# Additions to x on VectorE, one block sum to an item, and the first weights of a run split inside the run before it

## The chip, the cores and the metric

The kernel runs on one core of a Trainium2 chip. The metric is the device time of one execution in microseconds (us), the median of three runs for the kernel before. Five engines run side by side, each through its own list of instructions in order: TensorE (PE in the profile; its weight loads are PEld) multiplies into PSUM banks, VectorE (DVE) and ScalarE (ACT) work on SBUF and PSUM, GpSimd (POOL) works on SBUF and issues the DMAs that add while they write, SyncE (SP) issues the plain DMAs. Instructions of different engines wait for each other by semaphores.

## The reference

A two-layer encoder of 512 positions, width 1024, in float32. Each layer is attention and a SwiGLU feed-forward part, each behind an RMSNorm and added to x; a last RMSNorm ends it. Layer 0 has windowed attention with grouped keys, layer 1 a mixture of three dilated groups. The change touches the feed-forward part alone:

```
def swiglu(h, w_gate, w_up, w_down):
    return (jax.nn.silu(h @ w_gate) * (h @ w_up)) @ w_down

        h = rmsnorm(x, norm_ffn[i])
        x = x + swiglu(h, w_gate[i], w_up[i], w_down[i])
```

D_FF is 2816, which is 22 chunks of 128 hidden units. x is held transposed, as eight tiles of 128 features by 512 positions.

## The kernel before

**Products in three parts.** Every float32 operand is split into a high part in TensorE's rounded format and a low part, the rest (`split`, L92: ScalarE copies the high part, VectorE subtracts it from the source). A product is then three matmuls: high by high, high by low, low by high (`mm3`, L121; `product`, L738). A matmul has 128 rows of contraction, 128 outputs and 256 positions.

**The feed-forward part** is `swiglu` (L601). It runs twice, for layer 0 and for layer 1, with the same code:

- `conventional` (L892) makes hidden chunks 0 to 5 (PLAIN is 6) in the plain way.
- *Run 0* makes chunks 6 to 21 (L945): 16 items, each a gate and an up chunk together.
- *Run 1* (L946) multiplies chunks 6 to 13 by the down weights: four items of two output tiles of x (0 and 1, 2 and 3, 4 and 5, 6 and 7).
- *Run 2* (L947) does the same with chunks 14 to 21 for three items, output tiles 0 to 5.
- The *plain down products* (`down_plain`, L861) multiply chunks 0 to 5 for each of the eight output tiles; one tile is six chunk steps of six matmuls each. They come in three lots (L949): tiles 0 to 3 (24 chunk steps), 4 to 6 (18), and 7 (6). A lot begins at the end of a run and ends in the next.
- The *tail* (`tail`, L965) multiplies chunks 14 to 21 for output tiles 6 and 7 without the scheme below, with weights that `split_tail` (L985) prepares.

**An item** is a two by two block product done with seven block products rather than eight (the Strassen-Winograd scheme). Its operands on the side of the positions are B11, B21, B22 and the sums T1 to T4, made once for a run by `less` (VectorE, 1024 columns, L659) and split into the slots of bh and bl by `parts` (L655). On the side of the weights they are w1 to w7, made for every item by `weights` (L706). A pair of weights is loaded (`load_pair`, L701; SP); sums of weights are made by two plain DMAs and two accumulating ones (`load_sums`, L691; SP and GpSimd). From them come, by name: h12 and l12 (high and low parts of w1, w2), h64 and l64 (w6, w4), f5 and f7 (two sums on VectorE, 512 columns each, L725), h57 and l57 (w5, w7), `last` (a load of half a weight, L729), h3 and l3 (w3). The letters h are copies on ScalarE (L715), the letters l subtractions on VectorE (L721), of 1024 columns but for h3 and l3 with 512. The tiles wraw, wh and wl have three buffers each (L73), shared by pairs, by w1 w2, by w6 w4 and by the plain weights; the tile gs has two, and so has the sum of weights' h57 and l57; the sums have three.

**The order of work** is written out step by step in `strassens` (L811) and holds for TensorE, VectorE and ScalarE (L885, L990); the framework arranges SP and GpSimd. A step t has one block product. Item k's products w1 w2 w5 w4 w6 w3 w7 stand at steps 7k + 0, 1, 3, 5, 6, 9, 11, so neighbouring items interleave and each step of the middle has just one. The two banks of an item are a (tag mm, three buffers) and b (tag sc, two). Around the products, counted from the item's first step (L788):

- 1, 4, 7: ScalarE copies bank a to gs, to gs again, to us (L754); each copy must be done before the next product goes into bank a
- 8: `add`, VectorE adds part of bank b to us (L765), ahead of w7, which goes on in that part
- 12: `gate`, VectorE adds bank b to gs (L768); for a down item gs is then added to tile j of x: by GpSimd in run 1, by VectorE in run 2 (L774)
- 13: `both`, VectorE makes the other two blocks; for a down item it takes them into tile j + 1 of x (L785)

The weights of item k + 1 are made through item k's steps by the tables MAKE and MAKE_FIRST (L804, L808): for the second item of a run h12 at step 2, l12 and f5 at 3, f7 and h64 at 4, h57 and l64 at 5, l57 at 6, h3 at 10, l3 at 11; for later items h12 at the item's first step, l12 after it, then h64 and f5, l64, f7, h57, l57 at 2 to 6.

**Where runs meet** (from L1000). At the end of a run, steps without a product are filled with chunk steps of the plain lot that begins there: three at step `end`, then three at each of the last three steps (L849). The first weights of runs 1 and 2 are made after the last step, with chunk steps of the plain lot between them (eight ahead of run 1, four ahead of run 2, L1004 to L1011), and the rest of the lot (four, two) stands at step 2 of the new run (L839). The block sums of run 1 are made in the last steps of run 0 (L995 to L998), those of run 2 at steps 11, 14, 18 and 21 of run 1 (L1015). In `final` (L527), after the last layer, the tail's products are followed by the last norm and the outputs.

## Time and profile before

| | |
|---|---|
| median of three runs | 1389.37 us (1387.91 to 1391.34) |
| the profiled execution | 1389.48 us |
| its span, first to last instruction | 1387.7 us |
| mean granted TensorE clock | 0.998 |
| run 0's last step with w7 to the tail, layer 0 | from about 400 to 505 us |
| the same in layer 1 | from about 1259 to 1364 us |

The profile is that of one execution. A row of a timeline has the start, the duration, the engine, the line of the kernel, the operation and its tiles, output before input, and in brackets how long the engine had been idle before it and what ended that. Consecutive instructions of an engine overlap a little, so what one costs is read from start to start. A row of the waits view has the waiting engine and line, what it waited for, the total in us, the number of times and the longest. A row of the stretches has the busy time of each engine and its instructions, the granted clock and the DMA engines' share and GB/s. A row of the chain has a start, a duration and the work that the end of the kernel hung on there.

### The profile page before, as it was taken

What the parts mean: (1) busy time and instruction counts of PE and PEld (TensorE: products, weight loads), DVE (VectorE), ACT (ScalarE), POOL (GpSimd) and SP (SyncE); (2) the same over time, 40 slices, a digit from 0 to 9 for tenths busy, and PEclk for the clock granted to TensorE, in tenths of its full rate; (3) what the DMA queues carried; (4) which work ended last, traced back from release to release, by engine and by line L of the source; (5) the groups of instructions that cost most, each with busy time, mean ns of one, the idle gap of its engine ahead of it and who ended that gap; (6) DMA issues with size and microseconds to landing.
All of it is one profiled execution on the core that took longest, in us unless ns stands there. A gap on an engine that the chain in (4) does not pass through costs nothing.

```text
span 1387.7 us, 29649 instructions
## 1 busy us (share of the span) xinstructions
PE 1369.9 (99%) x12246; PEld 1352.1 (97%) x12246; DVE 960.0 (69%) x1699; ACT 726.7 (52%) x1304; POOL 262.2 (19%) x354
## 2 busy tenths in 40 slices
PE   9999999999999999999999999999999999999997
PEld 8988999999999999999999999999999999999997
DVE  6876558877779886345555555646466887778976
ACT  6766434555554567335545436436344555555543
POOL 1244220121202031011111111211132021210305
PEclk9999999999999999999999999999999999999999
DMA  6110263787747332322222122222136288774621
GB/s 204 62 62 16 77 176 103 188 204 186 191 134 183 103 104 78 108 79 91 70 84 91 64 92 78 77 84 70 63 107 175 92 213 199 189 194 137 169 88 62
DMA packets 67111, 164.63 MB, mean 119 GB/s; under 512 B 8992, under 2 KB 11424, under 8 KB 66976
## 3 DMA queue, kind: packets, MB, share of 16 engines
q1 hardware_dynamic: 51904, 137.95, 30.7%
q0 software_dynamic: 14784, 24.27, 10.8%
q8 instruction: 96, 1.57, 0.5%
q10 hardware_dynamic: 288, 0.52, 0.1%
q14 instruction: 39, 0.32, 0.1%
HBM read 160.53 MB, written 2.17 MB: 117 GB/s over the span
## 4 chain that ended last, share of the span: by engine, by line
PE 87%; DVE 6%; ACT 3%; issue 2%; DMA 1%; SPq 0%; POOL 0%; DVEq 0%; ACTq 0%; POOLq 0%
PE mm L126 31%; PE mm L742 16%; PE sc L742 12%; PE psv L126 9%; PE tp L126 6%; PE sc L126 2%; PE ov L447 1%; PE sc L1191 1%; PE ovb L1246 1%; PE sc L1132 1%; PE tp L1154 1%; ACT pr L423 1%; PE mm L973 1%; DVE pr L416 1%; PE ov L1173 1%
## 5 line engine op out<-in xcount | busy, mean ns | idle before, releaser
L98 DVE TENSOR_TENSOR wl<-wraw,wh 128x1024 fp32r<-128x1024 f32 (+4 forms) x154 | 179.2, 1166 | 106.8 <-ACT wh L97 103.9
L126 PE MATMUL mm<-xh,wh 128*128 128x256 f32 x1120 | 226.2, 283 | 0.5 <-ACT xh L260 0.5
L97 ACT ACTIVATE wh<-wraw 128x1024 fp32r<-128x1024 f32 (+4 forms) x153 | 149.3, 981 | 138.9 <-PE mm L126 101.3
L126 PE MATMUL mm<-xl,wh 128*128 128x256 f32 x1120 | 219.7, 278 | 0.3 <-DVE xl L261 0.3
L126 PE MATMUL mm<-xh,wl 128*128 128x256 f32 x1120 | 219.6, 277 | 0.0
L126 PEld LDWEIGHTS mm<-xh,wh 128*128 128x128 f32 x1120 | 169.9, 189 | 2.4 <-ACT xh L260 0.8
L126 PEld LDWEIGHTS mm<-xl,wh 128*128 128x128 f32 x1120 | 169.2, 188 | 1.0 <-DVE xl L261 1.0
L126 PEld LDWEIGHTS mm<-xh,wl 128*128 128x128 f32 x1120 | 169.0, 188 | 0.2 <-DVE wl L98 0.2
L698 POOL DMA_DIRECT2D w<-wunits x92 | 80.5, 918 | 442.7 <-DVE l L721 176.4
L742 PE MATMUL mm<-bh,h 128*128 128x256 f32 x368 | 102.3, 278 | 4.2 <-ACT gs L754 4.2
L742 PE MATMUL mm<-bh,l 128*128 128x256 f32 x368 | 102.3, 278 | 0.0
L742 PE MATMUL mm<-bl,h 128*128 128x256 f32 x368 | 102.0, 277 | 0.0
L742 PE MATMUL mm<-bl,wh 128*128 128x256 f32 x368 | 101.9, 277 | 0.0
L742 PE MATMUL mm<-bh,wl 128*128 128x256 f32 x368 | 101.9, 277 | 0.0
L742 PE MATMUL sc<-bh,wl 128*128 128x256 f32 x368 | 101.9, 277 | 0.0
L742 PE MATMUL sc<-bl,wh 128*128 128x256 f32 x368 | 101.9, 277 | 0.0
L742 PE MATMUL sc<-bh,wh 128*128 128x256 f32 x368 | 101.9, 277 | 0.0
L742 PE MATMUL mm<-bh,wh 128*128 128x256 f32 x368 | 101.9, 277 | 0.0
L126 PE MATMUL psv<-wh,xh 128*128 128x256 f32 x288 | 80.7, 280 | 0.0
L126 PE MATMUL psv<-wl,xh 128*128 128x256 f32 x288 | 79.9, 277 | 0.2 <-DVE wl L98 0.2
L126 PE MATMUL psv<-wh,xl 128*128 128x256 f32 x288 | 79.8, 277 | 0.0
L742 PEld LDWEIGHTS mm<-bh,h 128*128 128x128 f32 x368 | 69.3, 188 | 4.6 <-ACT gs L754 4.5
(250 smaller groups left out, 3955.7 us busy)
## 6 DMA issues: line engine op xcount, KB each, us to landing
wraw<-wunits SPq DMA_DIRECT2D x145, 512.0 KB, 3.3
w<-wunits SPq DMA_DIRECT2D x138, 256.0 KB, 3.7
w<-wunits POOLq DMA_DIRECT2D x92, 256.0 KB, 6.0
wraw<-wv SPq DMA_DIRECT2D x25, 512.0 KB, 3.4
wraw<-wunits SPq DMA_DIRECT2D x16, 384.0 KB, 4.1
x<-xT SPq DMA_DIRECT2D x8, 256.0 KB, 5.0
wraw<-wunits SPq DMA_DIRECT2D x3, 256.0 KB, 5.6
outT<-x SPq DMA_DIRECT2D x2, 384.0 KB, 2.8
```

The source lines that it names most:

```text
L97: nc.scalar.activation(out_h, src, AF.Copy)
L98: nc.vector.tensor_tensor(out_l, src, out_h.bitcast(F32), op=OP.subtract)
L126: nc.tensor.matmul(out[:, cols], a, b[:, cols], start=first and k == 0 and c == 0, stop=last and k == 2, skip_group_check=True)
L416: nc.vector.tensor_tensor_reduce(out=pr[:, e, :w], in0=ps[hf], in1=tab0[:, off:off + w], scale=SLOPES[heads[e]], scalar=-3e38, op0=OP.add, ...
L423: nc.scalar.activation(pr[:, e, :w + 1], pr[:, e, :w + 1], AF.Exp, bias=m[:, 1, e:e + 1], accum_out=m[:, 2, e:e + 1])
L447: nc.tensor.matmul(ov[64 * hf:64 * hf + 64, 256 * n:256 * n + 256], v0[:, k0 // 128 + kb, vs], st["pt", kb][:, 256 * hf:256 * hf + 256], s ...
L698: nc.gpsimd.dma_start(sums[:, 512 * k:512 * k + 512], v[:, 0:512], accum_op=OP.add)
L742: nc.tensor.matmul(out, a[:, j], b[:, j], start=first and j == 0 and i == 0, stop=j == 3 and i == 2, skip_group_check=True)
L973: nc.tensor.matmul(ps[:, 256 * h:256 * h + 256], a, (bl if low else bh)[:, slot, q % 4], start=q == 4 and k == 0 and 256 * h == cols.start ...
L1132: nc.tensor.matmul(out, qk["qs", p][a][:, 128 * t:128 * t + 128], kp[k], start=t == ts[0] and k == 0, stop=k == 1, skip_group_check=True)
L1154: nc.tensor.transpose(tp[:, (nb * a + kb) * 128:(nb * a + kb) * 128 + 128], st["pr", p, ts][:, a, o + 128 * kb:o + 128 * kb + 128], ident)
L1173: nc.tensor.matmul(ov[rows, 128 * t - 64:128 * t + 64], v[:, t - 1 + kb, vs], pt[:, 256 * a + 128 * kb:256 * a + 128 * kb + 128], start=Fa ...
```

## The change

1. For all down items the add of gs to x is on VectorE.
2. `both` of a down item stands at 10, right behind w3, instead of 13.
3. A plain lot loads and splits the weights of its first two products at its start and is then always two ahead; its second product goes to the bank with the tag ov.
4. At a run's end the chunk steps are spread: four at `end`, two at end + 3, two at each of the last three steps. Run 1 has six ahead of its first step and three each at steps 2 and 4; run 2 has none ahead and three each at steps 2 and 4.
5. Of a new run's first weights h12, l12, f5, f7, h57, l57, the load `last` and the split of T3 are made in the last five steps of the run before; h64, l64, h3, l3 stay between the runs.
6. T2 is formed as -B11 - T3 instead of -T1 - B22, so T3 comes first; for run 1 it is made at step 70 of run 0, and T4 and T1 in run 0's last steps. The sums of run 2 are made at steps 14, 21 and 23 of run 1, and the fourth between the runs. T4 and B22 are split at steps 4 and 6 of a run instead of 2 and 4. The tail's second weight is split one step earlier.

```
-                        eng = nc.vector if item[2] else nc.gpsimd
-                        eng.tensor_tensor(x[:, j, :], v["gs"], x[:, j, :], op=OP.add)
+                        nc.vector.tensor_tensor(x[:, j, :], v["gs"], x[:, j, :], op=OP.add)
...
+                if item[0] == "down":
+                    after[10] = after.pop(13)
...
                     if t == 2:
+                        for _ in range(3):
+                            next(lead, None)
+                    elif t == 4:
                         run(lead)
...
-                    if t == end or t > end + 4:
-                        for _ in range(3):
-                            next(left, None)
+                    for _ in range({end: 4, end + 3: 2}.get(t, 2 if t > end + 4 else 0)):
+                        next(left, None)
...
-                w = load_unit(wunits[at + js[0]][:, :128 * PLAIN], (PLAIN, 128))
+                def loaded(j):
+                    return load_unit(wunits[at + j][:, :128 * PLAIN], (PLAIN, 128))
+
+                w = [loaded(j) for j in js[:2]]
                 yield
                 for i, j in enumerate(js):
-                    (wh, wl), ps = w, bank("tp")
+                    (wh, wl), ps = w[i], bank("ov" if i == 1 else "tp")
...
-                        if c == 1 and i + 1 < len(js):
-                            w = load_unit(wunits[at + js[i + 1]][:, :128 * PLAIN], (PLAIN, 128))
+                        if c == 1 and i + 2 < len(js):
+                            w.append(loaded(js[i + 2]))
...
-                for k, step in ((1, first_set), (1, lambda: parts(B11, raw)),
-                                (3, lambda: less(raw, T1, B11, B12, raw[B11])), (4, lambda: parts(B21, raw)),
-                                (6, lambda: parts(T1, raw)), (9, lambda: less(raw, T2, T1, B22, raw[T1], -1.0)),
-                                (10, lambda: parts(T2, raw)), (13, lambda: less(raw, T3, B22, B12, raw[B12]))):
+                for k, step in ((-35, first_set), (-35, lambda: less(raw, T3, B22, B12, raw[B12])),
+                                (1, lambda: parts(B11, raw)), (2, lambda: less(raw, T2, B11, T3, raw[B11], -1.0)),
+                                (3, lambda: parts(B21, raw)), (5, lambda: parts(T2, raw)),
+                                (9, lambda: less(raw, T4, T2, B21, raw[B21], -1.0)),
+                                (10, lambda: less(raw, T1, T2, B22, raw[T2], -1.0)), (11, lambda: parts(T1, raw))):
                     others.setdefault(t + k, []).append(step)
...
                     if p:
-                        first, steps_ = weights(keys[p][0])
-                        steps_["T3"] = lambda: parts(T3, raw)
-                        for names in (("h12", "last", "l12", "f5"), ("f7", "h64", "l64"), ("T3",), ("h57", "l57"),
-                                      ("h3", "l3")):
-                            for m in names:
-                                steps_[m]()
-                            if names[0] != "h3":
-                                next(fill)
-                                if p == 1:
-                                    next(fill)
-                        lead, others = fill, {}
+                        for _ in range(6 if p == 1 else 0):
+                            next(fill)
+                        steps_of("h64", "l64")
+                        steps_of("h3", "l3")
+                        if p == 2:
+                            last_sum()
+                        first, lead, others = begun["w"], fill, {}
                     if p == 1:
-                        less(raw, T4, T2, B21, raw[T2], -1.0)
-                        others = {k: [step] for k, step in zip((11, 14, 18, 21), second_set())}
+                        *sums, last_sum = second_set()
+                        others = {k: [step] for k, step in zip((14, 21, 23), sums)}
...
-                                  t + 8: [lambda: split_tail(0)], t + 10: [lambda: split_tail(1)]}
+                                  t + 8: [lambda: split_tail(0)], t + 9: [lambda: split_tail(1)]}
                     if p:
-                        others.setdefault(2, []).append(lambda: parts(T4, raw))
-                        others.setdefault(4, []).append(lambda: parts(B22, raw))
+                        others.setdefault(4, []).append(lambda: parts(T4, raw))
+                        others.setdefault(6, []).append(lambda: parts(B22, raw))
+                    if p < 2:
+                        t = 7 * len(items)
+                        for k, step in ((3, lambda p=p: begin(p + 1)), (4, lambda: steps_of("h12", "last", "l12")),
+                                        (5, lambda: steps_of("f5", "f7", "h57")), (6, lambda: steps_of("l57")), (7, lambda: parts(T3, raw))):
+                            others.setdefault(t + k, []).append(step)
```

`begin` makes the weights' generator of the next run's first item, and `steps_of` issues its steps by name.

More of the change, by code (lines that the diff above doesn't have):

```diff
@@ L1000, in swiglu, with begin, steps_of @@
+                def begin(p):
+                    begun["w"], begun["steps"] = weights(keys[p][0])
+                def steps_of(*names):
+                    for m in names:
+                        begun["steps"][m]()
+                begun = {}
                 for p, items in enumerate(pairs):
                     if p:
-                        first, steps_ = weights(keys[p][0])
-                        steps_["T3"] = lambda: parts(T3, raw)
-                        for names in (("h12", "last", "l12", "f5"), ("f7", "h64", "l64"), ("T3",), ("h57", "l57"),
-                                      ("h3", "l3")):
-                            for m in names:
-                                steps_[m]()
-                            if names[0] != "h3":
-                                next(fill)
-                                if p == 1:
-                                    next(fill)
```

## The prediction

> **What bounds the kernel now.** I read the page first, then TensorE's waits, then busy time by stretch, then the chain that ended last, and last the timelines of VectorE and ScalarE around the waits.
>
> ```profile
> span 1387.7 us, 29649 instructions
> PE 1369.9 (99%) x12246; PEld 1352.1 (97%) x12246; DVE 960.0 (69%) x1699; ACT 726.7 (52%) x1304; POOL 262.2 (19%) x354
> ```
>
> TensorE is busy all through and the change takes no matmul away. So it can win only the idle time of TensorE, and what the changed stages hold of it is small. The waits view names it (total, times, longest, in us):
>
> ```profile
> PE mm L742 <- ACT gs L754: 4.2, 2, 2.1
> ...
> PE sc L742 <- DVE us L765: 1.1, 2, 0.6
> ```
>
> Each occurs twice, once in each layer. The stretches show where (busy us of PE with its matmuls, then of PEld, DVE, ACT, POOL, then PEclk):
>
> ```profile
> 250.00:400.00 150.00, 150.00 (x1326) 150.00 (x1325) 118.97 (x162) 86.37 (x130) 27.86 (x32) 1.00 0.80 195
> 430.00:465.00 35.00, 32.41 (x279) 31.99 (x279) 30.61 (x39) 15.01 (x22) 10.61 (x10) 1.00 0.65 165
> 465.00:515.00 50.00, 50.00 (x430) 50.00 (x429) 44.42 (x51) 30.22 (x40) 9.22 (x5) 1.00 0.27 91
> 1290.00:1325.00 35.00, 32.34 (x279) 31.91 (x278) 30.63 (x38) 14.71 (x21) 11.71 (x10) 1.00 0.63 159
> ```
>
> VectorE is the second engine: 30.61 of 35 us in the stretch that holds run 1. The chain tells the story of that stretch:
>
> ```profile
> 391.40 2.72 PE mm L742 x24
> ...
> 431.76 4.93 DMA w<-wunits
> ...
> 437.45 0.86 POOL w L698
> 438.31 1.30 POOL x L774
> ...
> 439.63 0.39 ACT gs L754
> ...
> 441.75 2.83 PE sc L742 x24
> ...
> 459.35 0.35 DVE us L765
> ```
>
> The add to x of item 0 of run 1 stands on GpSimd behind an accumulating weight DMA, which waits for a load. Until that add is done, gs can't be reused, ScalarE can't copy item 2's first sums out, and TensorE can't go on in that bank. Afterwards VectorE is late and the add of item 3 (L765) holds TensorE a second time.
>
> TensorE's normal pace is 2.72/24 = 0.1133 us a matmul. At it the 279 matmuls of 430 to 465 need 31.6 us; the stretch took 35. **Lost: 3.4 us, and as much in 1290 to 1325: 6.8 us.** That holds the waits, the pipeline's refilling and the pace of 2.83/24 = 0.1179 us after the longer wait. It is the ceiling of what the stalls can give back.
>
> **The change part by part.** At 0.1133 us a product of 12 matmuls takes 1.36 us, a chunk of a plain down product (6 matmuls) 0.68.
>
> *Adds to x.* Where the add is on VectorE already (run 2), and what it does to VectorE on GpSimd:
>
> ```profile
> L774 POOL TENSOR_TENSOR x<-gs,x x8: 1284/1438/2937, 438.0 to 1321.6; 128x512 f32<-128x512 f32 x8
> L774 DVE TENSOR_TENSOR x<-gs,x x6: 691/879/1729, 487.7 to 1362.9; 128x512 f32<-128x512 f32 x6
> ```
>
> ```profile
> 437.85 2.84 DVE L721 TENSOR_TENSOR wl<-wraw,wh 128x1024 fp32r<-128x1024 f32 x1
> ...
> 455.86 1.48 DVE L785 SCALAR_TENSOR_TENSOR x<-us,x 128x256 f32<-128x256 f32 x1
> ```
>
> ```profile
> 482.81 1.22 DVE L721 TENSOR_TENSOR wl<-wraw,wh 128x1024 fp32r<-128x1024 f32 x1
> 484.06 0.69 DVE L725 TENSOR_TENSOR wraw<-w,wraw 128x512 f32<-128x512 f32 x1
> 484.67 1.22 DVE L721 TENSOR_TENSOR wl<-w,wh 128x1024 fp32r<-128x1024 f32 x1
> 485.80 0.69 DVE L721 TENSOR_TENSOR l<-w,h 128x512 fp32r<-128x512 f32 x1
> 486.40 0.69 DVE L725 TENSOR_TENSOR wraw<-wraw 128x512 f32<-128x512 f32 x1
> 487.00 0.69 DVE L768 TENSOR_TENSOR gs<-sc,gs 128x512 f32<-128x512 f32 x1
> 487.73 0.69 DVE L774 TENSOR_TENSOR x<-gs,x 128x512 f32<-128x512 f32 x1
> 488.33 0.42 DVE L785 SCALAR_TENSOR_TENSOR x<-mm,x 128x256 f32<-128x256 f32 x1
> 488.67 0.41 DVE L785 SCALAR_TENSOR_TENSOR x<-us,x 128x256 f32<-128x256 f32 x1
> 489.00 1.22 DVE L721 TENSOR_TENSOR l<-wraw,h 128x1024 fp32r<-128x1024 f32 x1
> 490.14 0.42 DVE L765 TENSOR_TENSOR us<-sc,us 128x256 f32<-128x256 f32 x1
> ```
>
> From start to start this last fence gives what each operation costs VectorE: 1.14 for 1024 columns (1.25 where a sum that overwrites its input follows), 0.60 for 512, 0.67 for `both`, 0.73 from `gate` to its dependent add. So an added add costs 0.60 + 0.13 = 0.73 us, 2.9 for the four of a layer. GpSimd's adds stretched VectorE's work by 2.84 - 1.22 = 1.62 and 1.48 - 0.42 = 1.06 us in this layer: 2.7 go. For VectorE the move is even, and the wait behind the DMA is gone with its 2.2 us a layer. The longest row, 1.73, would make it 4 us dearer a layer, the bound on that side.
>
> *Order of sums.* T3 moves to step 70 of run 0 (1.14 us, in a run where VectorE has 150 - 119 = 31 us free over 16 items); T2 is formed from T3. Without that cover it would cost 1.14 a layer. The second set's sums keep their number, the last moves behind the run. I take nothing.
>
> *First weights in the last steps, plain chunks between products, `both` at 10.* The number of chunks is the same (24, 18, 6); only their places change: TensorE's own time stays. VectorE's and ScalarE's order is written out, so I walk it with the costs above. In run 0's end it starts from B11's low part:
>
> ```profile
> 391.49 1.23 DVE L98 TENSOR_TENSOR bl<-acts_xh,bh 128x1024 fp32r<-128x1024 f32 x1 [1.59 <-ACT bh L97]
> ```
>
> Four operations of 1.14 (B11, T2's sum, B21, T2's low part), three plain low parts of 768 columns (0.87 each, between the other sizes), two of 0.60, `both`, 1.7 of waiting for ScalarE's copies, and 0.42 for `add` of item 15: it ends at 402.6. TensorE, from the row at 391.40, has five products, four chunks, w3 and two chunks ahead of w7: 403.6. It fits by 1.0. The other bank for the second plain product, and `both` three steps earlier, remove no wait that the list has: nothing by themselves. The moved loads (R0's pair and last half, the second plain weight) go earlier on SP's queue; the sums of item 3 are requested when l64 of item 0 is done, which I place 3 us later than now:
>
> ```profile
> wraw<-wunits SPq DMA_DIRECT2D x145, 512.0 KB, 3.3
> w<-wunits SPq DMA_DIRECT2D x138, 256.0 KB, 3.7
> w<-wunits POOLq DMA_DIRECT2D x92, 256.0 KB, 6.0
> ```
>
> By the walk below l64 ends some 5 us into run 1; 3.7 + 6.0 and two issues of 0.9 make it 17; they are wanted at step 16, 23 us in. GpSimd has nothing but these DMAs left in these steps, so a late load there holds nobody else up. No cost.
>
> *The starts of runs 1 and 2* decide. Weights' tiles wh, wl have three buffers, in the order of first writing. In run 1 the order is P0 P1 P2 R0(1,2) P3 R0(6,4) R1(1,2): item 1's first copy takes the buffer of R0(1,2), free early. In run 2 there are three plain products: P0 P1 P2 Q0(1,2) Q0(6,4) Q1(1,2): item 1's first copy takes P2's buffer, and P2's last chunks now stand at step 4. ScalarE waits for TensorE there, as it does today at other places, and everything behind it in its order waits too: the second copy of item 0's sums, which w6 needs (1.06 + 0.38 after the wait, against 1.36: just in time), and the copies of h64, T4, h57 and B22.
>
> ```profile
> 467.32 1.06 ACT L715 ACTIVATE wh<-w 128x1024 fp32r<-128x1024 f32 x1 [3.02 <-PE tp L126]
> 468.28 1.04 ACT L97 ACTIVATE bh<-acts_xh 128x1024 fp32r<-128x1024 f32 x1
> ```
>
> Count from the end of step 4's chunks. TensorE does w4 w6 and item 1's w1 w2, then w3 (5 x 1.36 = 6.80), then w5 of item 1, whose low part is wanted at its third matmul, 7.03; w7 at 8.16; w2 of item 2 at 13.6.
> - Run 1: l12 and f5 are done before; ScalarE copies h64 and T4 (0.95 + 1.06), so T4's low part starts at 2.05; then l64, l57: the latter ends at 2.05 + 2 x 1.14 + 1.22 = 5.55; B22's and `add`: 2.05 + 4 x 1.14 + 0.42 = 7.03; on through l12, f5, both, l64, l3, f7 (1.25 + 0.60 + 0.67 + 1.14 + 0.60 + 0.60 = 4.86, from 6.95) gate ends at 12.5. Spare: 1.5, 1.1, 1.1 us.
> - Run 2: first the copy h12 (1.06 and 0.04 to hand over), then l12 1.25, f5 0.60, the plain product's add 0.60, f7 0.60: T4's low part starts at 4.15, 2.1 later. Spare: -0.6, -1.0, -1.0. **TensorE stands for 1.0 us a layer**, in two pieces (w5, then w7).
>
> Lower bound 0 (the copy finds another buffer); upper bound 2.1 + 1.0, if VectorE has work left when the copy comes.
>
> **Sum.** 6.8 of stalls go, 2 x 1.0 come: 4.8. The profiled execution took 1389.48 us (1.8 beside its span, unchanged), 0.1 from the median of 1389.37. 1389.5 - 4.8 = **1384.7 us**.
>
> *TensorE's two paces.* The rows of TensorE have 0.1133 us a matmul in 250 to 400 and 50/430 = 0.1163 on average in 465 to 515; from 474 it is 0.118:
>
> ```profile
> 477.14 2.83 PE mm L742 x24
> ...
> 553.29 23.14 PE psv L126 x204
> ```
>
> At 553 it is 0.1134 again, with the granted clock at 1.00 throughout. From 474 to 553 the slow pace costs 79 x (1 - 0.1133/0.1179) = 3.1 us. It starts after some waits of TensorE and not after others, so the change, which shifts all waits, can switch it. [...]
>
> **Rivals.**
> - *Fast pace in layer 0.* After a short stop of 0.7 us (at 459) TensorE went on fast. If it does so after the new stop, 3.1 go too: 1381.6. Against: at 474 it turned slow without a listed wait. 0.20.
> - *No new stop.* The copy of item 1 finds a free buffer: 1382.7. For: I infer the order of the buffers from the code and no row names them; against: ScalarE's waits above follow it. 0.13.
> - *The lag reaches the tail.* Six chunks (4.1 us) that stood ahead of run 2 stand inside it now, so its VectorE work begins later against TensorE; the low parts of the tail's weights are made last, and today just in time in layer 0:
>
> ```profile
> 503.59 2.27 DVE L98 TENSOR_TENSOR wl<-wraw,wh 128x1024 fp32r<-128x1024 f32 x1
> ```
>
> ```profile
> 505.40 0.71 PE mm L973 x6
> ```
>
> The second of them ends at 505.86, after the tail has begun. The last l57, on which the last plain weight's load hangs, ends 505.40 - 490.22 = 15.2 us before the tail now; by the walk it ends 16.5 after the count's start, and the tail begins 29.6 after it (16 products, 6 chunks, w3 and w7, and the stop): 13.1. If these 2.1 us go through to the tail in layer 0 and half of them in layer 1, where it has more room, 3.2 go back: about 1387.9. 0.18.
> - *Slower.* One mechanism: the slow pace sets in early, at run 0's end, where the added chunks shift TensorE, and holds to the end of the layer. From 398 to 440 and 450 to 474 that is 66 us, in layer 1 from 1257 to 1370 some 100 more: 166 x 0.039 = 6.5 us against 4.8: 1391.2. If it begins at step 70, 57 us earlier a layer, it is 4.4 more: 1395.6. It decides from 4.8/0.039 = 123 us of added slow pace. Against: those stretches run fast today in both layers. 0.07.
>
> **How the numbers follow.** The forecast (1384.7, give or take 1.2 for the walk) has 0.42. The bound of what can be measured here is 0.3%, 4.2 us: 1385.2. Below it lie some 0.6 of the forecast's share (0.25), nearly all of the fast pace (0.19) and of the case without a stop (0.11): 0.55. Over 1393.5 lies half of the slow case and a bit for waits I don't see: 0.07. Within: 0.38. The range of 8 in 10 reaches from the fast pace with a little of the stop gone, 1380.8, to beyond the tail's case, 1388.6.
>
> **What would show it.** Right: no wait of TensorE on ACT gs L754; no add of L774 on GpSimd; in run 1 no wait at all; in run 2 a wait of about 0.6 us at item 1's w5 (on DVE l) and one of 0.4 at w7 (on DVE us), after a long wait of ScalarE's copy for the plain product. Wrong: a stop in run 1 (VectorE dearer than its rows), a stop at the tail's first matmuls, weight loads that TensorE waits for, or a pace other than today's from 474 to 553 or after 1309.

## The result and the profile after

| | before | after |
|---|---|---|
| median on the same occasions | 1389.03 us (1387.91 to 1391.34) | 1381.21 us (1380.10 to 1382.53, four runs) |
| ratio after to before | | 0.9942 (95% interval 0.9925 to 0.9959) |
| the profiled execution, its span | 1389.48 us, 1387.7 us | 1382.53 us, 1380.8 us |

The changed kernel is faster by 7.8 us, by the interval 5.7 to 10.4. The forecast was 1384.7: the measured time lies 3.5 us below it, and 0.4 us inside the low end of the range of 8 in 10. The gain of 7.8 us is 3.0 over the 4.8 of the sum.

The page of the changed kernel begins so (busy us, share of the span, instructions):

```profile
span 1380.8 us, 29630 instructions
PE 1365.4 (99%) x12246; PEld 1348.7 (98%) x12246; DVE 958.3 (69%) x1707; ACT 725.8 (53%) x1304; POOL 248.1 (18%) x346
```

The work is the same: 12246 matmuls, and VectorE's 960 us have become 958. TensorE's waits (total, times, longest) in the changed kernel:

```profile
PE sc L979 <- DVE wl L98: 1.9, 1, 1.9
PE ssq L278 <- ACT tmp L271: 1.5, 1, 1.5
...
PE psv L126 <- DVE wl L98: 1.0, 2, 0.8
```

Both waits on which the prediction rested are gone: none on ACT gs L754, none on DVE us L765. Two others stand there, L979 (the tail, L973 before) and psv (the first products of layer 1's attention). The stretches of the changed kernel (busy us of PE with its matmuls, of PEld, DVE, ACT, POOL, then the granted clock):

```profile
430.00:465.00 35.00, 35.00 (x311) 35.00 (x310) 33.12 (x45) 16.85 (x24) 5.21 (x6) 1.00 0.64 175
465.00:515.00 50.00, 48.10 (x424) 47.91 (x423) 43.44 (x50) 30.08 (x40) 7.76 (x5) 1.00 0.26 85
515.00:560.00 45.00, 44.19 (x369) 43.98 (x368) 28.11 (x55) 30.67 (x57) 6.09 (x5) 0.96 0.32 99
1290.00:1325.00 35.00, 35.00 (x311) 35.00 (x310) 33.11 (x44) 19.21 (x27) 3.46 (x4) 1.00 0.67 180
```

Where 279 matmuls ran in 35 us, 311 run now. The view also counts those that reach over an edge of the stretch; by their starts it is 277 and 308, and 308 is what fits at 0.1133 us. The stretch from 515 has lost clock (0.96).

All kernels but the one with small matmuls have the same number of matmuls, so two executions can be laid beside each other by count: the time from the start of matmul number a to that of number b. This table is worked out in that way from the start times in the traces (us); the edits of its columns follow below.

```
stretch (matmuls)                  before  again   adds  adds   adds   after  after  tail   chunks copy   tail +
                                                   alone again  back          again  early  back   waits  layer 1
attention's end, 0   1160-1520      42.22  40.94  40.94  40.94  42.35  42.22  40.94  40.94  40.94  40.94  40.94
run 0, layer 0       1520-3400     213.22 213.36 213.37 213.36 213.19 213.07 213.19 213.19 214.73 213.19 213.19
run 1, layer 0       3400-3960      67.34  67.55  64.31  64.34  63.47  63.47  63.47  63.47  64.34  63.47  63.47
run 2, layer 0       3960-4240      32.91  32.98  32.91  32.91  31.73  31.73  31.77  31.91  32.98  33.00  31.73
tail, layer 0        4240-4340      11.78  11.78  11.78  11.78  15.14  13.52  13.94  11.78  13.05  12.34  11.33
start of layer 1     4340-4680      39.75  39.75  39.75  39.75  38.66  42.00  39.39  44.09  39.04  43.11  42.54
attention's end, 1   9040-9400      42.35  42.35  40.98  42.35  42.35  40.98  42.35  42.35  40.98  42.35  40.98
run 0, layer 1       9400-11240    208.77 208.78 208.76 208.77 208.60 208.60 208.60 208.60 210.13 208.62 208.60
run 1, layer 1      11240-11800     67.41  66.81  65.96  65.96  63.47  63.47  63.47  63.47  63.89  63.47  63.47
run 2 to the end    11800-12246     53.01  54.61  55.34  54.22  52.59  53.23  53.64  53.53  52.65  54.00  52.58
```

After minus before, row by row: 0, -0.2, -3.9, -1.2, +1.7, +2.3, -1.4, -0.2, -3.9, +0.2, in all -6.5 of the 6.9 us between the two spans. The row "attention's end, 1" lies outside the change: it is 42.35 in seven of the eleven and 40.98 in four, and the changed kernel has given both. That -1.4 is chance, and so is the like in "attention's end, 0". Four entries hold some us at half clock: 15.14 (the additions back; a mean granted clock of 0.97 from 465 to 515 us), 42.00, 44.09 and 43.11 (0.68, 0.52 and 0.50 from 528 to 532 us).

### The profile page after: what moved, and what is told of

It is laid out like the page before. It is cut to its first block, busy times and chain, and to the rows that moved or that the text cites. A ratio compares the mean times of both kernels' runs of the same rounds, so it can differ in the third digit from the quotient of the medians.

```text
span 1380.8 us, 29630 instructions
## 1 busy us (share of the span) xinstructions
PE 1365.4 (99%) x12246; PEld 1348.7 (98%) x12246; DVE 958.3 (69%) x1707; ACT 725.8 (53%) x1304; POOL 248.1 (18%) x346
## 4 chain that ended last, share of the span: by engine, by line
PE 90%; DVE 5%; ACT 3%; issue 1%; DMA 1%; SPq 0%; POOL 0%; DVEq 0%; ACTq 0%
PE mm L126 30%; PE mm L742 17%; PE sc L742 13%; PE psv L126 10%; PE tp L126 6%; PE sc L126 2%; PE ov L447 1%; PE ov L126 1%; PE sc L1207 1%; PE ovb L1262 1%; PE sc L1148 1%; DVE wl L98 1%; PE tp L1170 1%; ACT pr L423 1%; DVE pr L416 1%
## 5 line engine op out<-in xcount | busy, mean ns | idle before, releaser
L1239 POOL TENSOR_SCALAR pr<-pr,mb 128x256 f32<-128x256 f32 x64 | 38.3, 611 | 182.9 <-DVE mb L1232 180.4
```

The costliest lines, as they stand in the source:

```text
L1239: nc.gpsimd.tensor_scalar(of(pr[:, a, :], c), of(pr[:, a, :], c), den[:, c % 2, a:a + 1], 1.0, op0=OP.mult, op1=OP.mult)
```

## The experiments

Each was timed against the kernel before on the same occasion, but for the three single executions in part 8.

**1. The additions alone.** The kernel before with

```
-                        eng = nc.vector if item[2] else nc.gpsimd
-                        eng.tensor_tensor(x[:, j, :], v["gs"], x[:, j, :], op=OP.add)
+                        nc.vector.tensor_tensor(x[:, j, :], v["gs"], x[:, j, :], op=OP.add)
```

> Kernel before with one edit: in run 1 the additions to x are on VectorE; order of sums, weights and plain chunks as before. Theory (the add that stood behind a weight DMA on GpSimd made the first stall, and order has little to do with it): the wait of TensorE on ACT gs at L754 goes in both layers (4.2 us of wait), VectorE loses 4 x 0.6 us of added work a layer and gets back some 2.7 us of stretching; the stretch 430 to 465 us runs some 305 matmuls where 279 ran before and 311 fit; the short second wait on DVE us at L765 (0.6 us a layer) may stay; time 1389.0 less 4 to 6 us, 1383 to 1385. Rival A (the reordering is what removes the stall, VectorE is late without it): the wait moves from ACT gs to DVE us or DVE l in run 1 with at least 1.5 us a layer, and the time is within 2 us of 1389. Rival B (the additions are the whole change): 1381 to 1382, the time of the full change, with neither wait left.

Measured: 1383.78 us (1381.0 to 1385.16), ratio 0.9963 (0.9951 to 0.9975): 4.9 us. Its waits and stretches:

```profile
PE sc L742 <- DVE us L765: 0.2, 1, 0.2
```

```profile
430.00:465.00 35.00, 34.79 (x306) 34.58 (x305) 31.75 (x44) 16.59 (x23) 4.73 (x6) 1.00 0.65 170
...
1290.00:1325.00 35.00, 35.00 (x300) 35.00 (x299) 30.66 (x41) 16.70 (x24) 3.46 (x4) 1.00 0.57 153
```

The theory held in its first half: the long wait goes, 306 matmuls run, and of the second wait (0.6 us a layer) 0.2 is left in one layer. The second line shows what it keeps of the loss: TensorE never stops, and yet only 300 matmuls run in 35 us (297 by their starts, 0.1178 us each). That is the slow pace; it holds there from 1255 us to the end of run 2.

**2. The additions back.** The changed kernel with the same two lines the other way round.

> Changed kernel with one edit undone: the additions to x in run 1 are back on GpSimd; everything else as changed. Theory: GpSimd takes the addition behind an accumulating weight DMA again, so TensorE waits on ACT gs at L754 once more, 1 to 2.1 us a layer, and VectorE is stretched by about 2.7 us a layer; time 1381.2 plus 3 to 6 us, 1384 to 1387. Rival A (the new order asks for the sums so much earlier or later that the addition no longer stands behind a DMA that is waiting): no wait on L754, time 1381 to 1382. Rival B (the gain came from the reordering): the same, no loss over 1 us.

Measured: 1381.16 us (1380.07 to 1382.38), ratio 0.9949 (0.9937 to 0.9960), the time of the full change. My theory fell. GpSimd in the kernel before, at the first addition of run 1:

```profile
431.19 1.76 POOL L698 DMA_DIRECT2D w<-wunits  x2 [10.10 <-DVE wraw L725]
437.45 0.86 POOL L698 DMA_DIRECT2D w<-wunits  x1 [4.50 <-DMA w<-wunits]
438.02 1.58 POOL L774 TENSOR_TENSOR x<-gs,x 128x512 f32<-128x512 f32 x1
```

and in this run:

```profile
430.63 1.76 POOL L698 DMA_DIRECT2D w<-wunits  x2 [6.67 <-DVE wraw L725]
433.74 1.29 POOL L774 TENSOR_TENSOR x<-gs,x 128x512 f32<-128x512 f32 x1 [1.35 <-DVE gs L768]
439.36 1.78 POOL L698 DMA_DIRECT2D w<-wunits  x2 [4.33 <-DMA w<-wunits]
```

The wait for the load is there in both (4.50 and 4.33 us). Before, the addition stands behind it; in the new order the sums are asked for later, and the addition is done 4 us before the weight DMA's turn. So either half of the change removes the stall by itself: an addition on VectorE has nothing in front of it, and an addition on GpSimd with the new order has nothing in front of it either. VectorE's work is still stretched beside GpSimd's additions (l57, 1.22 us, takes 1.87 here), and its order now has the room: run 1 takes 63.47 us with them and without.

**3. The changed kernel again.**

> The changed kernel without any edit, once more, for what recurs from one execution to another: the wait of 1.9 us at the tail of layer 0, the half granted clock for 3.4 us at 527 us, the fast pace of 0.1133 us a matmul from 474 to 530 us and from 1010 to 1045 us. Theory (pace and clock follow from the waits of the program): all four recur within 0.2 us and the time is 1381.2 give or take 1. Rival (pace and clock fall out by chance in each execution): the pace of 474 to 530 or the half clock differ, and times of single executions spread by 2 to 4 us.

Measured: 1380.31 us (1379.75 to 1381.26), ratio 0.9943 (0.9931 to 0.9955). The wait at the tail recurred with 1.9 us, runs 1 and 2 of layer 0 and runs 0 and 1 of layer 1 to 0.04 us, run 0 of layer 0 to 0.12. The half clock at 527 us didn't (the granted clock is 1.00 from 515 to 560 us), the pace behind the tail's stop was slow this time (13.94 for 13.52), and the attention's ends were 40.94 and 42.35 where they had been 42.22 and 40.98. So the theory holds for the runs and the tail's stop, the rival for the clock and for the pace outside the runs.

**4. The tail's second weight a step earlier**, in the changed kernel:

```
-                                  t + 8: [lambda: split_tail(0)], t + 9: [lambda: split_tail(1)]}
+                                  t + 8: [lambda: split_tail(0), lambda: split_tail(1)]}
```

> Changed kernel with the second weight of the tail split at the same step as the first (one step earlier). Theory (TensorE stands 1.9 us before the tail of layer 0 because VectorE has the operand of x, stretched to 2.0 us by GpSimd's squares, ahead of this low part): the wait on DVE wl L98 at the tail falls from 1.9 us to under 0.3 us; the time falls by 1 to 2 us, to 1379 to 1380, the smaller end if the start of layer 1, where VectorE is late too, takes part of it back. Rival A (the wait is for the tail's weight in general, VectorE is simply behind with its whole order there): the wait stays over 1 us or turns up on DVE x or xl, time within 0.5 us of 1381.2. Rival B (layer 1's start is the bound whatever comes before it): the wait at the tail goes, and a wait of the same size grows at psv L126, time 1381.

Measured: 1381.92 us (1380.23 to 1384.42), ratio 0.9952 (0.9940 to 0.9964). VectorE ahead of the tail, first in the changed kernel, then here:

```profile
497.79 2.29 DVE L98 TENSOR_TENSOR wl<-wraw,wh 128x1024 fp32r<-128x1024 f32 x1
500.00 2.03 DVE L261 SCALAR_TENSOR_TENSOR xl<-x,g_sb,xh 128x512 fp32r<-128x512 f32 x1
501.95 1.21 DVE L98 TENSOR_TENSOR wl<-wraw,wh 128x1024 fp32r<-128x1024 f32 x1
```

```profile
497.67 2.34 DVE L98 TENSOR_TENSOR wl<-wraw,wh 128x1024 fp32r<-128x1024 f32 x2
499.94 2.07 DVE L261 SCALAR_TENSOR_TENSOR xl<-x,g_sb,xh 128x512 fp32r<-128x512 f32 x1
```

The second low part ends at 500.0 instead of 503.2, and the wait at the tail is gone (11.78 us in the table, as before the change). And then, in TensorE's waits of this run:

```profile
PE psv L126 <- DVE wl L98: 1.8, 2, 1.6
```

The 1.9 us come back 25 us later as a wait of 1.6, where the changed kernel's two profiles have 0.8 and 0.2: rival B. At the start of layer 1 VectorE makes eight operands of x and two weights on end (in the changed kernel):

```profile
519.77 5.91 DVE L261 SCALAR_TENSOR_TENSOR ol<-x,g_sb,oh 128x512 fp32r<-128x512 f32 x6
525.61 1.22 DVE L98 TENSOR_TENSOR wl<-wraw,wh 128x1024 fp32r<-128x1024 f32 x1
```

**5. The start of layer 1 in another order**, on top of experiment 4: the low part of the values' first weight behind the fourth operand, that of the second behind the sixth, the norm's row three steps later.

```
+        v_first = v_unit(0, 0, apart_=True)[1]
...
+            for j in range(2, 6):
+                operands(2, j, oh, ol)
+                if j == 3:
+                    next(v_first)
+            run(gens[0])
+            next(v_first)
+            for j in range(6, NK):
+                operands(2, j, oh, ol)
...
-        spread([3, lambda: norm_rows(at=4)], gens[0])
+        spread([6, lambda: norm_rows(at=4)], gens[0])
```

> Changed kernel with the tail's second weight a step earlier, as in the run before of that edit, and with the start of layer 1 in another order: VectorE makes the low part of the first weight of the values behind the fourth operand of x and that of the second behind the sixth, where it made all eight operands first, and the row of the norm is turned three steps later. Theory (the start of layer 1 hangs on VectorE's order; with the tail's stop gone it lost 1.6 us at psv, and 3.4 us of half clock with it): no wait over 0.3 us at psv L126, none at the tail, no half clock there; against the run with the tail's edit alone 2 to 5 us less: 1377 to 1379.5. Rival A (VectorE has too much to do there in whatever order): the wait at psv turns into one on DVE ol of the same 1 to 1.6 us, time 1381 to 1382. Rival B (the half clock comes from the one-column matmuls of the norm and not from the stop): the wait goes and 3.4 or 6.8 us of half clock stay, time 1379 to 1381.

Measured: 1380.29 us (1379.84 to 1381.24), ratio 0.9942 (0.9929 to 0.9954), no better than the changed kernel's second set of runs. Its waits keep

```profile
PE psv L126 <- DVE wl L98: 1.0, 2, 0.9
PE mm L126 <- DVE xl L265: 0.6, 1, 0.6
```

and the table has 42.54 us from 4340 to 4680, without any half clock (granted 1.00 from 515 to 560 us), where the changed kernel needs 39.39 without one. The 2.6 us that the tail's row gains on the changed kernel's second profile (11.33 for 13.94) are paid back there in full. What stays open is whether an order exists in which VectorE gets through; this one is not it.

**6. The plain chunks at a run's end as before**, in the changed kernel:

```
-                    for _ in range({end: 4, end + 3: 2}.get(t, 2 if t > end + 4 else 0)):
+                    for _ in range(3 if t == end or t > end + 4 else 0):
                         next(left, None)
```

> Changed kernel with the plain chunks at a run's end placed as before (three at step end, none at end + 3, three at each of the last three steps, twelve in all as now). Theory of the prediction's walk (the add of item 15 ends 1.0 us before w7 wants it, with the three chunks that now stand ahead): TensorE reaches w7 of item 15 three chunks, 2.0 us, earlier and waits 1.0 us for DVE us there, and up to 0.3 us at the end of run 1, in each layer: 1381 plus 2.0 to 2.6, 1382.5 to 1384. Rival A (VectorE has at least 2 us of room there): no wait over 0.2 us at run 0's end and no change of the time. Rival B (the stop also turns TensorE to its slow pace for the rest of the runs, 0.0046 us for each of some 700 matmuls): 3 us more in a layer where it happens, up to 1387.

Measured: 1385.47 us (1382.8 to 1389.28), ratio 0.9983 (0.9973 to 0.9992): 2.4 us of the change's 7.8 are left. Its waits, and the matmul that waits at run 0's end:

```profile
PE sc L742 <- DVE us L765: 2.4, 2, 1.2
```

```profile
401.86 0.39 PE L742 MATMUL sc<-bh,h 128*128 128x256 f32 x1 [1.21 <-DVE us L765]
```

The walk had given 1.0 us; it is 1.2, once in each layer. The rest by the table: 1.5 a layer, as the matmuls around the wait of 1.21 us start 1.48 and 0.22 us apart where 0.11 is usual; a gap of 0.4 us in run 1 of layer 0, after which the slow pace holds to the tail (0.9 and 1.3); 0.4 in run 1 of layer 1; and 0.5 back at the tail, where TensorE, being later, waits less. Theory and rival B together.

**7. The copy that should have waited.** The prediction took 2.0 us for a wait of item 1's copy h12 at the start of run 2. In the changed kernel ScalarE does this:

```profile
457.84 1.06 ACT L715 ACTIVATE wh<-wraw 128x1024 fp32r<-128x1024 f32 x1 [3.14 <-PE tp L126]
464.77 1.04 ACT L715 ACTIVATE wh<-w 128x1024 fp32r<-128x1024 f32 x1
...
466.50 1.05 ACT L715 ACTIVATE wh<-wraw 128x1024 fp32r<-128x1024 f32 x1
469.62 0.39 ACT L754 ACTIVATE gs<-mm 128x256 f32<-128x256 f32 x1 [2.08 <-PE mm L742]
471.44 1.06 ACT L715 ACTIVATE wh<-w 128x1024 fp32r<-128x1024 f32 x1 [1.43 <-PE tp L126]
```

The first two lines are item 0's copies h12 (from wraw) and h64 (from w), the others item 1's. Item 1's h12 doesn't wait; its h64, two places later, is the one that waits for the plain product, with nothing urgent behind it. To bring the predicted case about, I first had the tiles of h64 taken ahead of those of h12 (in run 2):

```
+                def place64():
+                    t[6, 4] = [wpool.tile([128, 1024], F32R, name=m) for m in ("wh", "wl")]
...
+                    if not t and not then:
+                        at(2, steps["p64"])
```

> Changed kernel with one edit: in run 2 the tiles wh, wl for h64 of item 1 are taken before those for h12, so that it is h12 that gets the buffer of the last plain product before it and waits for the plain chunks of step 4. This is the case that the prediction took for its sum. Theory of the prediction's walk: TensorE stands for 0.6 us at w5 of item 1 (on DVE l) and 0.4 us more at w7 (on DVE us) in each layer, 2.0 us in all, and the time is 1381 plus 2, 1382.5 to 1383.5. Rival A (the walk is right and the lag goes on to the tail of layer 0): besides, the wait on DVE wl L98 at the tail grows from 1.9 us by about 1 us: 1384. Rival B (ScalarE and VectorE have more room there than the walk gives them): no wait over 0.2 us in run 2 and the time of the changed kernel, 1380 to 1381.5.

Measured: 1381.05 us (1379.24 to 1382.21), ratio 0.9943 (0.9930 to 0.9957). The edit missed its aim: the copy from wraw stands at 465.37 without a wait, the copy from w at 470.31 waits 1.43 us. By this a buffer is given at the first writing, not where the tile is taken. So this run says nothing of the walk. The second attempt puts the copy itself first:

```
+                    first_of = MAKE_FIRST if then else {**MAKE_FIRST, 2: ("h64", "h12"), 4: ("f7",)}
-                    for k, names in (MAKE if t else MAKE_FIRST).items():
+                    for k, names in (MAKE if t else first_of).items():
```

> Changed kernel with one edit: in run 2 the copy h64 of item 1 stands ahead of h12, so that h64 takes the free buffer and h12 the one of the last plain product (the edit of the tiles alone left the copy h12 where it was, without a wait). Now the prediction's case should be there: h12 waits for the plain chunks of step 4, and the copy of item 0's second sums stands behind it. Theory of the prediction's walk: TensorE stands 0.6 us at w5 of item 1 and 0.4 us more at w7 in each layer, 2.0 us in all: 1381 plus 2, 1382.5 to 1383.5, and the tail's wait of layer 0 stays at 1.9 us or shrinks as TensorE is later. Rival A (l64's work is done early in exchange, so VectorE makes the lost time good): a stop of less than 0.4 us a layer, 1380.5 to 1381.8. Rival B (the sums of item 1 have not landed at that time, and ScalarE waits for them first): a longer wait of ScalarE on a DMA, stops of over 1 us a layer, 1383.5 to 1386.

Measured: 1383.60 us (1381.84 to 1385.85), ratio 0.9958 (0.9945 to 0.9972), by the ratios 2.2 us over the changed kernel. ScalarE, then the matmul that waits, then TensorE's waits in sum:

```profile
465.75 1.05 ACT L715 ACTIVATE wh<-w 128x1024 fp32r<-128x1024 f32 x1
470.69 1.06 ACT L715 ACTIVATE wh<-wraw 128x1024 fp32r<-128x1024 f32 x1 [3.88 <-PE tp L126]
471.66 0.36 ACT L754 ACTIVATE gs<-mm 128x256 f32<-128x256 f32 x1
...
474.97 1.06 ACT L715 ACTIVATE h<-wraw 128x1024 fp32r<-128x1024 f32 x1 [2.00 <-DVE wraw L725]
...
476.88 0.36 ACT L754 ACTIVATE us<-mm 128x256 f32<-128x256 f32 x1
```

```profile
477.30 0.38 PE L742 MATMUL mm<-bh,h 128*128 128x256 f32 x1 [0.72 <-ACT us L754]
```

```profile
PE mm L742 <- ACT us L754: 1.4, 2, 0.7
```

Now the case is there. Run 2 takes 1.27 us more in each layer (33.00 for 31.73 in the table, and 35.27 for 34.00 from 11800 to 12100); the walk had 1.0. The stop stands at another place: VectorE is late with f7, ScalarE's copy of h57 waits 2.00 us for that, and item 0's last copy of sums (us), which w3 needs, stands behind it. So VectorE's lag reaches TensorE through ScalarE, one product ahead of where the walk saw it. In layer 0 the tail gives 1.2 us back (12.34 for 13.52), so that 1.3 of the two layers' 2.5 is left, which the interval of the 2.2 holds.

**8. The pace of TensorE.** The kernel before and experiment 1's kernel, each in one more execution:

> The kernel before without any edit, for a second profile of it. For the question which of its stretches of slow pace belong to it. Theory (the pace is settled by the stops, and the same stops leave the same pace): the stop of 2.1 us in run 1 is followed by 0.118 us a matmul to the next stop in both layers as before, and the stretch from 474 to 527 us is slow again; 1010 to 1045 us may differ. Rival (chance): at least one of these three is at 0.113 this time. The two waits of run 1 recur in any case: 4.2 us on ACT gs, 1.1 us on DVE us; 1387 to 1391.

> The kernel before with the additions on VectorE alone, a second profile. In the first the slow pace set in at 1255 us in layer 1 after a gap of 0.16 us and held for 100 us, which cost some 4 us; in layer 0 the same stretch was fast from 404 to 470. Theory (chance decides after such a gap): at least one of the two layers differs from the first profile, and the time lies anywhere from 1381 to 1385.5. Rival (the program settles it): slow from 1255 us again, fast from 404 to 470, slow from 470, within 1383 to 1385.

Measured: 1389.16 and 1386.42 us. In the kernel before the stops themselves vary a little from execution to execution: GpSimd's first addition of run 1 starts at 436.34 us now, behind a weight DMA ahead of which GpSimd was idle for 4.35 us, where it was 438.02 and 4.50 (3.0 us in four waits on ACT gs now, where 4.2 in two were):

```profile
PE mm L742 <- ACT gs L754: 3.0, 4, 1.8
...
PE sc L742 <- DVE us L765: 1.1, 2, 0.6
```

and the pace behind them differs: in run 1 of layer 0 it turned slow at 458 us and not at 440, and run 2 of layer 1 was slow where the first profile had it fast. From 474 to 527 us it was slow again. So the rival of chance holds for the kernel before. Experiment 1's kernel, in which no addition waits for a DMA, repeats every row of the runs to 0.03 us, the 100 us of slow pace in layer 1 among them: it sets in at the same matmul, after a gap of 0.16 us in both. In these two profiles the program settles it; the difference of the two executions, 1386.42 against 1384.38, lies outside the runs.

To see what sets it, one execution of the changed kernel with a small matmul ahead of each item of run 0 but the first.

```
+                    if q == 0 and 0 < i < len(items) == 16:
+                        nc.tensor.matmul(bank("ov")[:, 0:1], ident, ones, start=True, stop=True)
```

> Changed kernel with one small matmul (128 by 1 output, into a free bank, nobody reads it) ahead of each item but the first in run 0, 15 in each layer: 30 small breaks in the even row of matmuls. For the question of what sets TensorE's pace of 0.1133 or 0.1179 us. Theory (each break in the row draws the pace anew, and it holds to the next break): of the 30 stretches of 84 matmuls some run at 0.113 and some at 0.118, at least three of each; time 1381 plus 30 times some 0.1 to 0.2 us for the breaks plus 0.39 us for each slow stretch, 1384 to 1395. Rival (the pace belongs to the stage or to longer waits): all 30 stretches at 0.113 as without the breaks; 1384 to 1387.

Measured: 1387.82 us. My theory fell: all 30 stretches went on at 0.1133 us. Its stretch of run 0, in which 30 of the records are those of the small matmuls, has no slow part:

```profile
250.00:400.00 150.00, 150.00 (x1326) 150.00 (x1325) 117.80 (x159) 85.16 (x128) 27.89 (x32) 1.00 0.78 191
```

A small matmul costs 0.22 us (gaps of 0.026, 0.112 and 0.200 for one of 0.113). It didn't change the pace here; behind the gap of 0.16 us in experiment 1's layer 1 the slow pace came.

## Why the prediction was right or wrong

The time lies inside the range, near the rivals of the fast pace (1381.6) and of no new stop (1382.7), and not where the sum put it. That it does is in part luck: the stop of 2.0 us that didn't come and the one of 1.9 us at the tail nearly cancel.

- **The ceiling of the stalls** (6.8 us): right in kind, 1.0 too small. Run 1's rows give back 3.9 us in each layer, 7.8 in all. Of each layer's missing 0.5, 0.2 lies at the run's beginning, outside the stretches that the prediction counted, and 0.2 to 0.3 comes of its count: by their starts 277 and 276 matmuls ran in the two stretches and not 279.
- **The additions**: the rule of cost was right (0.69 us each, and no new wait of TensorE on VectorE; experiment 1), the role was not. The prediction put the end of the first stall down to them and took the new order to remove no wait by itself. Experiment 2 shows that the new order does it as well. The sum doesn't change by that, since both halves were in the change.
- **Order of sums, loads, `both`**: no cost taken, none found; TensorE doesn't wait for a load in the runs.
- **Run 0's end**: the walk had `add` of item 15 end at 402.6; it ends at 402.78, and experiment 6 shows the room: 1.2 us are missing without the moved chunks, where the walk had 1.0.
- **Run 1**: no wait, as walked.
- **Run 2**: wrong, and this is the step that failed: "Weights' tiles wh, wl have three buffers, in the order of first writing". The writing has that order, but by the waits in experiment 7 a copy gets the buffer that is released first, not the next one around. No view names the buffers; item 1's h12 starts at 466.50 us without a wait, so it took that of w1 and w2 of item 0, released after w2, and h64 behind it had to wait for the plain product's. The 2.0 us didn't come. The second edit of experiment 7 (the copy that waits) shows that the price was about right, 1.27 a layer for 1.0, with the stop one product earlier, at ScalarE's copy us. So the rival without a new stop was the case, which had 0.13 where the forecast had 0.42.
- **The lag at the tail**: there in layer 0, 1.9 us of wait where the rival had 2.1, but only in part by its mechanism (six chunks more inside run 2, VectorE later against TensorE). By the start times the tail's first matmul stands at 505.24 us before and at 500.02 now, and the last l57 ends 15.0 us ahead of it before and 14.2 now: 0.8 us of lag and not 2.1. In layer 1 it is 14.0 and 14.2, no lag, and no wait. But the second low part ends 0.6 us after that matmul before and 3.1 now; the other 1.7 us of these 2.5 arise behind l57. One operand of x more (1.04 us from start to start) stands ahead of the first low part now, and the rest is work of VectorE that takes longer than before. Before:

```profile
499.06 1.14 DVE L261 SCALAR_TENSOR_TENSOR xl<-x,g_sb,xh 128x512 fp32r<-128x512 f32 x1
500.13 0.40 DVE L765 TENSOR_TENSOR us<-sc,us 128x256 f32<-128x256 f32 x1
500.46 1.20 DVE L98 TENSOR_TENSOR wl<-wraw,wh 128x1024 fp32r<-128x1024 f32 x1
501.59 2.08 DVE L261 SCALAR_TENSOR_TENSOR xl<-x,g_sb,xh 128x512 fp32r<-128x512 f32 x1
```

  and in the changed kernel, just ahead of the three lines in experiment 4:

```profile
495.37 1.14 DVE L261 SCALAR_TENSOR_TENSOR xl<-x,g_sb,xh 128x512 fp32r<-128x512 f32 x1
496.42 0.41 DVE L765 TENSOR_TENSOR us<-sc,us 128x256 f32<-128x256 f32 x1
496.75 1.14 DVE L261 SCALAR_TENSOR_TENSOR xl<-x,g_sb,xh 128x512 fp32r<-128x512 f32 x1
```

  So the rival's size agrees in good part by luck. That it stood among the rivals and not in the sum was the second error, of opposite sign and of the same size.
- **The pace**: run 2 of layer 0 is fast now (-1.2 us in the table), in both profiles of the changed kernel. The rival had 3.1, with the fast pace to 553 us; behind the tail's stop it went on to the next layer's first products, about 523 us, in the one profile and ended at 502 in the other. Both paces stand at a granted clock of 1.00: in 1290 to 1325 us, most of it run 1 of layer 1, experiment 1's kernel has 300 matmuls without a stop, the changed kernel 311, at 117.8 and 113.3 ns a matmul.
- **Not seen at all**: the start of layer 1. It is full for VectorE (8.00 of 8 us busy from 520 to 528 us in the changed kernel), so a part of what layer 0 gains is lost there: 0.8 us of wait in the changed kernel's first profile (0.2 in its second), 1.6 when the tail's stop is taken away.

In sum for the profiled execution, from the table: 7.8 (stalls) + 1.2 (pace) + 0.3 (run 0) - 1.7 (tail) - 2.3 (start of layer 1, of which 1.7 is half clock) + 1.4 (chance, outside) - 0.2 (the end) = 6.5. That execution took 1382.53 us, 1.3 over the median; the half clock, which is not in every execution, is 1.7 of it.

## What to carry to other kernels

Before a stall is put down to one cause, ask what else in the change moves the blocked instruction or the one in front of it: here two halves of a change each removed the same stall, and only undoing them one at a time showed it. Where a pool hands out buffers, look up in the trace which release a copy waits for, before a wait is priced. Follow a gain to the next stretch in which the second engine is full: 1.9 us taken from the tail came back as 1.6 at the next layer's start.

## What the runs showed of the hardware

**Two paces that mostly keep themselves.** TensorE has 0.1133 or 0.1178 us a matmul of 256 columns at a granted clock of 1.00. By the start times in the traces, a matmul starts 110 ns after its weight load started at the fast pace and 114 to 115 at the slow one. Either mostly goes on until the next stop, but not always: at 474.5 us in the kernel before and at 495.7 in experiment 4, where a block product follows plain chunks, one matmul starts 14 to 16 ns late (129 ns behind the one ahead of it, where 113 is usual, in the kernel before) without any wait in the trace, and the slow pace sets in behind it. Which pace a stop leaves behind wasn't settled: the same stop of 1.9 us at the tail left the fast one in the changed kernel's first profile and the slow one in its second.

**Half the clock near short stops.** Granted clock of the changed kernel around the stop at psv, and of experiment 4 around its longer one:

```profile
524.00:528.00 4.00, 3.19 (x24) 2.98 (x24) 4.00 (x7) 2.67 (x4) 0.00 (x0) 0.89 0.06 13
528.00:532.00 4.00, 4.00 (x26) 4.00 (x26) 2.02 (x7) 0.82 (x3) 0.00 (x0) 0.68 0.93 272
```

```profile
524.00:528.00 4.00, 2.36 (x14) 2.15 (x14) 3.93 (x8) 2.22 (x3) 0.00 (x0) 0.63 0.10 26
528.00:532.00 4.00, 4.00 (x21) 4.00 (x21) 1.49 (x4) 0.60 (x1) 0.00 (x0) 0.52 0.83 286
```

The loss is 4 x (0.11 + 0.32) = 1.7 us and 4 x (0.37 + 0.48) = 3.4 us, so 3.4 and 6.8 us at half clock (in the changed kernel it is 0.50 from 528 to 530 us). It came beside stops of 0.8 to 1.9 us between 500 and 540 us in five executions (the changed kernel's, experiments 2, 4 and the two of 7) and not in four others (experiments 3, 5, 6 and the small matmuls), the same 1.9 us at the tail among both. That the stops set it off isn't shown. In experiment 4 the stop of 1.6 us ends at 526.47 us, and the clock falls almost as it begins:

```profile
524.00:525.00 1.00, 0.83 (x7) 0.62 (x6) 1.00 (x2) 1.00 (x1) 0.00 (x0) 1.00 0.00 0
525.00:526.00 1.00, 0.00 (x0) 0.00 (x0) 1.00 (x2) 0.07 (x1) 0.00 (x0) 0.52 0.00 0
```

And of the 35 executions of the kernel before that were timed beside the experiments, nine have a mean clock of 0.995 or 0.996; of the profiled executions only some of those with such a half clock have so little, and those without it have 0.997 or 0.998.
